# Down projection in two halves of four output tiles, with its end done tile by tile, in an autoregressive trunk on one core

## The chip, the cores and the metric

The kernel runs on one core of a Trainium2 chip. What counts is the device time of one execution in microseconds (us). Time before: 927.52 us, the median of three runs (925.98 to 929.55). Lower is better.

## What is computed

A two-layer residual trunk on 256 tokens of width 1024. Each layer is: half an FFN, a mixer, half an FFN. All FFNs are SwiGLU with an inner width of 2816. The mixer of layer 0 is latent attention beside a causal pooling mixer; that of layer 1 is a spatial gate (gMLP).

```
def _rmsnorm(x, g):
    y = x * lax.rsqrt(jnp.mean(x * x, axis=-1, keepdims=True) + EPS)
    return y * g
def _swiglu(x, w_gate, w_up, w_down):
    return (jax.nn.silu(x @ w_gate) * (x @ w_up)) @ w_down

cos, sin = _rope_tables(positions)
for layer in range(DEPTH):            # DEPTH = 2
    h = h + 0.5 * _swiglu(_rmsnorm(h, ffn_norm[layer, 0]), ...)
    hn = _rmsnorm(h, mix_norm[layer])
    if layer % 2 == 0:                # q, k, v from low rank; 8 heads; pooling; one output projection
        h = h + _mla_pool_mixer(hn, cos, sin, ...)
    else:                             # u, v = gelu(hn @ w_in); (u * mixed(v)) @ w_out
        h = h + _spatial_gating_mixer(hn, ...)
    h = h + 0.5 * _swiglu(_rmsnorm(h, ffn_norm[layer, 1]), ...)
```

## The kernel before

**Layout.** Everything is held transposed: the residual `hT` (in the trace `par_h`) has 8 tiles of 128 features by 256 tokens. Every weight passes through the core once, in chunks of 128 partitions by 1024 values (512 KB; a few are smaller). The chunks stand in one list, in the order of their use. Each is loaded into one of 5 `raw` buffers by SyncE (SP), rounded by ScalarE (ACT) to `whi` (L165), and VectorE (DVE) makes the rest `wlo = raw - whi` (L173). There are 6 pairs of `whi` and `wlo` (`PAIRS`), so a seventh chunk can be rounded only when TensorE (PE) is done with the first. Five chunks are split by GpSimd (POOL) instead.

**Matmuls.** A product with a weight is made of a rounded part and a rest on both sides. In the FFNs (`mm2`, L207 and L208) one tile of weights takes two matmuls, one of 256 columns and one of 512, the latter giving two half results in one PSUM bank. The mixers use three of 256 columns or more (`mm3`, L201 to L203). Each bank of a tile is one of eight: four in a set named `acc`, four in a set named `rot`, each set handed out in turn.

**An FFN** (`ffn`) has 11 blocks of 4 chunks in `gate_up`, which fill four banks from the normed input `x` (L207/L208 `<-x`). Blocks of even number use `acc`, of odd number `rot`. `evacuate` (L345 on ACT, L347 on DVE) and `epilogue` (L355 to L361) turn the banks into `pp`, the input of the down projection. The down stage has 22 chunks, one for each block of 128 inner features (k), each with all 8 output tiles (m), in all 8 banks: tiles 0 to 3 in `rot`, 4 to 7 in `acc`. The last two k are done tile by tile. Then `finish` adds each tile to the residual (`add`, two DVE instructions at L390), and makes from it the next stage's input: `norm_hi` (ACT, L256) and `norm_lo` (DVE, L259) write the two parts of tile m of the next `x`, `norm_sq` (ACT, L264) and POOL (L269) sum the squares. In the last FFN each tile is added and sent out instead.

**Mixers.** `even_mixer` collects its output projection in four `acc` banks, two tiles in a bank. It goes through a list `todo` of (k, m) and fills it in between the steps of attention; `pair_out` turns two heads' values (PE transposes at L858), and ACT (L859) and DVE (L860) write them as the next k of `comb`. `odd_mixer` does its output projection k by k, with all 8 tiles in four `acc` banks. Both end with `finish`, whose add is one DVE instruction at L306.

**Order.** The program's order on each engine is the order in which the Python code is written; every engine goes through its own list in order. `next_chunk` issues the loads, roundings and splits of chunks to come (three ahead, `LOOK`). `rope_tables` (L417 to L455) makes the rotary tables with some 30 small DVE instructions and a sine on ACT, after block 6 of the first FFN's gate/up stage.

## Time and profile before

| what | value |
|---|---|
| median of three runs | 927.52 us |
| the profiled execution | 928.45 us, span 926.3 us from first to last instruction |
| PE busy | 903.3 us, 98% of the span |
| DVE busy | 649.3 us, 70% |
| ACT busy | 498.2 us, 54% |
| mean granted PE clock | 0.989 |
| moved from HBM | 162.5 MB, 177 GB/s over the span |

A busy PE is not a PE at its peak: matmuls overlap, and at half clock PE counts as busy for twice as long. So the places of interest are found by the granted clock, by PE's waits, and by the distance from one matmul's start to the next. "x" with a number behind a row is its count. In a row of the timeline stand start, duration, engine, line, operation, result and inputs, and in brackets the idle time before it with what ended it.

### The profile page before, as it was taken

To read this page: it belongs to the slowest core of one execution; us is meant where nothing else is said; L and a number is where in the kernel's file an instruction comes from. 1 tells how busy PE (TensorE), PEld (TensorE's weight loads), DVE (VectorE), ACT (ScalarE), POOL (GpSimd) and SP (SyncE) were. 2 spreads that over 40 slices of the span, in tenths; PEclk is the share of its full clock that TensorE was granted. 3 is DMA by queue.
4 is the path that set the end of the run, shared out by engine and by line. 5 is a ranking of instruction groups with operands and counts; after the bars stand their busy time and mean duration, and the time that the engine had idled before them with its cause. 6 is when DMAs were issued, how large, how long until landed. Compare 5 with 4: busy or idle time off the path is not lost.

```text
span 926.3 us, 13892 instructions
## 1 busy us (share of the span) xinstructions
PE 903.3 (98%) x5320; PEld 793.7 (86%) x5320; DVE 649.3 (70%) x973; ACT 498.2 (54%) x782; POOL 98.9 (11%) x130
## 2 busy tenths in 40 slices
PE   8999899999999999999989999999999899999998
PEld 6888788889888888888878888888899888888886
DVE  7787876479875877774477777754768658777643
ACT  7555455358673655553354555543555546555430
POOL 4200000027433000000031000000220220000000
PEclk9999999999998999999989999999999999999999
DMA  8575456525353555556524555575356455555741
GB/s 284 191 248 191 135 197 239 183 88 177 114 160 114 164 193 199 194 200 228 186 93 166 198 182 183 182 242 188 98 191 207 127 167 192 182 188 199 249 137 45
DMA packets 48017, 164.45 MB, mean 178 GB/s; under 512 B 5456, under 2 KB 7760, under 8 KB 47952
## 3 DMA queue, kind: packets, MB, share of 16 engines
q1 hardware_dynamic: 47952, 163.58, 53.0%
q8 instruction: 41, 0.67, 0.3%
q14 instruction: 24, 0.20, 0.1%
HBM read 162.51 MB, written 1.05 MB: 177 GB/s over the span
## 4 chain that ended last, share of the span: by engine, by line
PE 88%; DVE 7%; POOL 1%; ACT 1%; issue 1%; DMA 1%; SPq 0%; DVEq 0%; POOLq 0%; ACTq 0%
PE acc L208 27%; PE rot L208 24%; PE acc L207 14%; PE rot L207 12%; PE acc L202 2%; PE acc L201 2%; PE acc L203 2%; DVE par_h L390 2%; DVE x L259 2%; PE rot L202 1%; PE rot L203 1%; PE rot L201 1%; DMA raw<-w_gu 1%; DVE wlo L173 1%; DVE par_h L306 1%
## 5 line engine op out<-in xcount | busy, mean ns | idle before, releaser
L173 DVE TENSOR_TENSOR wlo<-raw,whi 128x1024 fp32r<-128x1024 f32 (+2 forms) x298 | 353.8, 1229 | 102.0 <-ACT whi L165 101.9
L165 ACT CAST whi<-raw 128x1024 fp32r<-128x1024 f32 (+2 forms) x303 | 303.2, 1043 | 144.0 <-PE acc L208 117.2
L208 PE MATMUL acc<-x,whi 128*128 128x512 f32 x768 | 275.3, 401 | 0.0
L207 PE MATMUL acc<-x,wlo 128*128 128x256 f32 x768 | 219.0, 285 | 10.4 <-DVE par_h L306 4.5
L208 PE MATMUL rot<-x,whi 128*128 128x512 f32 x640 | 225.4, 396 | 0.0
L207 PE MATMUL rot<-x,wlo 128*128 128x256 f32 x640 | 179.3, 280 | 3.3 <-DVE wlo L173 3.3
L208 PEld LDWEIGHTS acc<-x,whi 128*128 128x128 f32 x768 | 147.5, 192 | 34.0
L207 PEld LDWEIGHTS acc<-x,wlo 128*128 128x128 f32 x768 | 148.0, 193 | 15.1 <-DVE par_h L306 6.7
L208 PEld LDWEIGHTS rot<-x,whi 128*128 128x128 f32 x640 | 120.7, 189 | 28.2
L208 PE MATMUL acc<-pp,whi 128*128 128x512 f32 x352 | 127.3, 396 | 0.0
L208 PE MATMUL rot<-pp,whi 128*128 128x512 f32 x352 | 127.3, 396 | 0.0
L207 PEld LDWEIGHTS rot<-x,wlo 128*128 128x128 f32 x640 | 121.1, 189 | 3.6 <-DVE wlo L173 3.6
L207 PE MATMUL acc<-pp,wlo 128*128 128x256 f32 x352 | 99.0, 281 | 0.0
L207 PE MATMUL rot<-pp,wlo 128*128 128x256 f32 x352 | 98.9, 281 | 0.0
L208 PEld LDWEIGHTS acc<-pp,whi 128*128 128x128 f32 x352 | 66.1, 188 | 16.0
L208 PEld LDWEIGHTS rot<-pp,whi 128*128 128x128 f32 x352 | 66.1, 188 | 15.9
L347 DVE TENSOR_TENSOR gu<-acc,a 128x256 f32<-128x256 f32 x96 | 34.2, 417 | 46.6 <-ACT a L345 46.4
L207 PEld LDWEIGHTS rot<-pp,wlo 128*128 128x128 f32 x352 | 66.3, 188 | 0.0
L207 PEld LDWEIGHTS acc<-pp,wlo 128*128 128x128 f32 x352 | 66.3, 188 | 0.0
L345 ACT COPY a<-acc 128x256 f32<-128x256 f32 x96 | 32.8, 372 | 62.1 <-PE acc L208 62.1
L269 POOL TENSOR_TENSOR sqsum<-sq,sq 128x256 f32<-128x256 f32 x6 | 4.6, 772 | 535.1 <-ACT sq L264 535.1
L356 ACT ACTIVATE gu<-gu 128x512 f32<-128x512 f32 x44 | 27.9, 634 | 50.5 <-DVE gu L355 50.5
(237 smaller groups left out, 1037.0 us busy)
## 6 DMA issues: line engine op xcount, KB each, us to landing
raw<-w_gu SPq DMA_DIRECT2D x172, 512.0 KB, 4.7
raw<-w_down SPq DMA_DIRECT2D x88, 512.0 KB, 4.5
raw<-ew_out SPq DMA_DIRECT2D x8, 512.0 KB, 4.0
raw<-ow_v SPq DMA_DIRECT2D x8, 512.0 KB, 3.6
raw<-ow_u SPq DMA_DIRECT2D x8, 512.0 KB, 5.1
raw<-ow_out SPq DMA_DIRECT2D x8, 512.0 KB, 4.4
raw<-ew_p SPq DMA_DIRECT2D x4, 512.0 KB, 3.9
raw<-w_gu SPq DMA_DIRECT2D x7, 256.0 KB, 5.2
```

What stands on the lines that cost most here:

```text
L165: nc.scalar.copy(hi[:, :n], r[:, :n])
L173: eng.tensor_sub(lo[:, :n], r[:, :n], hi[:, :n].bitcast(F32))
L201: nc.tensor.matmul(out, wl, xh, start=start, stop=False, skip_group_check=True)
L202: nc.tensor.matmul(out, wh, xl, start=False, stop=False, skip_group_check=True)
L203: nc.tensor.matmul(out, wh, xh, start=False, stop=stop, skip_group_check=True)
L207: nc.tensor.matmul(bank[:, 0:T], wl, x[:, 1, :], start=start, stop=False, skip_group_check=True)
L208: nc.tensor.matmul(bank, wh, x.rearrange("p s t -> p (s t)"), start=False, stop=stop, skip_group_check=True)
L259: nc.vector.scalar_tensor_tensor(s.xl[:, k, :], hT[:, k, :], pcol(s.gname, s.goff + k), s.xh[:, k, :].bitcast(F32), op0=ALU.mult, op1=ALU. ...
L345: nc.scalar.copy(a[:, i, :], bank[:, 0:T])
L347: nc.vector.tensor_add(gu[:, i, :], bank[:, T:], a[:, i, :])
L356: nc.scalar.activation(t, t, AF.Silu)
L390: nc.vector.tensor_add(hT[:, m, :], half, hT[:, m, :])
```

## The change

- **Down in halves.** A chunk of `w_down` now holds two k and four output tiles (two runs of 2 KB in a partition instead of one of 4 KB). All 11 chunks of tiles 0 to 3 come first, then the 11 of tiles 4 to 7. Each half needs four banks.
- **Bank sets dealt anew.** Each FFN is told which set its even blocks use. Half 0 takes the set of the odd blocks, half 1 that of the even blocks, and the next stage starts with the set of half 0.
- **The end tile by tile.** `finish` is cut into steps. Steps 0 to 3 are issued in half 1 after its chunks 0 to 3. The last three chunks (6 k) are fetched together (`next_chunks`, which holds back the rounding of chunks that would need one of these three's buffers), and done tile by tile with a step behind each tile. In the last FFN the steps add and send out.
- **Mixers.** In `odd_mixer` the last three k are done tile by tile, with two steps behind each second tile. In `even_mixer` what is left of `todo` after the last `pair_out` is sorted by tile, and the last k looks three chunks ahead instead of four; `finish` follows as before.
- **Rotary tables** are made in the down stage of the first FFN, after chunk 3 of half 0.

```diff
     def ffn_chunks(li):
         gu = [[w_gu[li, b, c] for c in range(4)] for b in range(NB)]
-        dn = [[w_down[li, b, j] for j in range(2)] for b in range(NB)]
-        return sum(gu, []) + sum(dn, [])
+        dn = [w_down[li, b, :, :, h * 512 : (h + 1) * 512].rearrange("j p n -> p j n")
+              for h in range(2) for b in range(NB)]
+        return sum(gu, []) + dn
...
-            while st["hi"] < min(max(st["split"] + 2, HEAD), len(chunks)):
+            while st["hi"] < min(max(st["split"] + 2, HEAD), cap or len(chunks), len(chunks)):
                 emit_hi()
...
+    def next_chunks(n, k):
+
+        cap = st["use"] + PAIRS
+        return [next_chunk(k, min(LOOK, PAIRS - 1 - i), cap) for i in range(n)]
...
+    def finisher(add, nxt):
+
+        def step(m):
+            if m < KD:
+                add(m)
+                norm_hi(nxt, m)
+            if m > 0:
+                norm_lo(nxt, m - 1)
+                norm_sq(nxt, m - 1)
+        return step
...
-    def ffn(s, nxt_args, first=False):
+    def ffn(s, nxt_args, sets, first=False):
...
-                new = rot_bank if b % 2 else acc_bank
-                banks = [new() for _ in range(4)]
+                banks = [sets[b % 2]() for _ in range(4)]
...
-                if first and b == 6:
-                    rope_tables()
...
-            ws = [next_chunk(1) for _ in range(3)]
-            for ms in (range(4), range(4, KD)):
-                for k in range(3):
-                    for m in ms:
-                        down(k, m, ws[k])
-            for k in range(3, K - 2):
-                w = next_chunk(1)
-                for m in range(KD):
-                    down(k, m, w)
-            ws = [next_chunk(1), next_chunk(1)]
-            for m in range(KD):
-                for j in range(2):
-                    down(K - 2 + j, m, ws[j])
...
+            for hf in range(2):
+                ms = range(4 * hf, 4 * hf + 4)
+                for m in ms:
+                    banks[m] = sets[1 - hf]()
+                for b in range(NB - 3 * hf):
+                    w = next_chunk(2)
+                    for j in range(2):
+                        for m in ms:
+                            down(2 * b + j, m, w)
+                    if hf == 1 and b < 4:
+                        step(b)
+                    if first and hf == 0 and b == 3:
+                        rope_tables()
+            ws = next_chunks(3, 2)
+            for m in range(4, KD):
+                for k in range(K - 6, K):
+                    down(k, m, ws[(k - K + 6) // 2])
+                step(m)
+            step(KD)
...
-            look_of = {7: 1, 6: 1, 5: 2, 4: 3, 0: 3, 1: 3, 2: 4, 3: 4}
+            look_of = {7: 1, 6: 1, 5: 2, 4: 3, 0: 3, 1: 3, 2: 4, 3: 3}
...
+            todo.sort(key=lambda t: t[1])
             fill(2 * KD * 4)
             finish(lambda m: residual(accs, m), nxt)
...
-            for k in range(KD):
+            for k in range(KD - 3):
...
+            ws = next_chunks(3, 1)
+            for m in range(KD):
+                for k in range(KD - 3, KD):
+                    out_tile(accs, m, ws[k - KD + 3], (zh[:, k, :], zl[:, k, :]), False, k == KD - 1)
+                if m % 2:
+                    step(m - 1)
+                    step(m)
+            step(KD)
...
-    s = ffn(s, ("mix", 0), first=True)
+    s = ffn(s, ("mix", 0), (acc_bank, rot_bank), first=True)
     s = even_mixer(s, ("ffn", KD))
-    s = ffn(s, ("ffn", 2 * KD))
-    s = ffn(s, ("mix", KD))
+    s = ffn(s, ("ffn", 2 * KD), (rot_bank, acc_bank))
+    s = ffn(s, ("mix", KD), (acc_bank, rot_bank))
     s = odd_mixer(s, ("ffn", 3 * KD))
-    ffn(s, None)
+    ffn(s, None, (rot_bank, acc_bank))
```

**How instructions move, three places.** First DVE where the rotary tables begin, before, in the gate/up stage (a row: line, operation, result from inputs, size; the numbers in names are buffers):

```order
L347 TENSOR_TENSOR gu_987<-acc_898,a_988 128x256
L355 TENSOR_TENSOR gu_987<-gu_987,rb_388 128x512
L357 TENSOR_TENSOR gu_987<-gu_987,rbh_390 128x512
L358 TENSOR_TENSOR gu_987<-gu_987 128x512
L361 TENSOR_TENSOR pp_212<-gu_987,pp_212 128x2x256
L419 CAST posi_1003<-pos_i 128x2
L423 TENSOR_SCALAR ang<-cst_sb,posi_1003 128x16 x2
```

The same on DVE now, in the down stage:

```order
L375 TENSOR_TENSOR pp_212<-gu_1419,pp_212 128x2x256
L177 TENSOR_TENSOR wlo_1398<-raw_1293,whi_1397 128x1024
L177 TENSOR_TENSOR wlo_1441<-raw_1335,whi_1440 128x1024
L177 TENSOR_TENSOR wlo_1463<-raw_1357,whi_1462 128x1024
L177 TENSOR_TENSOR wlo_1485<-raw_1379,whi_1484 128x1024
L435 CAST posi_1528<-pos_i 128x2
L439 TENSOR_SCALAR ang<-cst_sb,posi_1528 128x16 x2
```

Before, the tables stood right behind an epilogue, with four splits behind them; now four splits stand between the last epilogue and the tables, and only splits follow.

Second PE at the step from the second FFN's down stage (`<-pp`) to the third FFN's gate/up stage (`<-x`), before:

```order
L207 MATMUL acc_4265<-pp_3052,wlo_4619 128x256
L208 MATMUL acc_4265<-pp_3052,whi_4618 128x512
L207 MATMUL acc_4265<-pp_3052,wlo_4641 128x256
L208 MATMUL acc_4265<-pp_3052,whi_4640 128x512
L207 MATMUL acc_4817<-x_4257,wlo_4663 128x256
L208 MATMUL acc_4817<-x_4257,whi_4662 128x512
L207 MATMUL acc_4818<-x_4257,wlo_4663 128x256
L208 MATMUL acc_4818<-x_4257,whi_4662 128x512
```

The same on PE now:

```order
L216 MATMUL rot_4507<-pp_3046,wlo_4644 128x256
L217 MATMUL rot_4507<-pp_3046,whi_4643 128x512
L216 MATMUL rot_4507<-pp_3046,wlo_4666 128x256
L217 MATMUL rot_4507<-pp_3046,whi_4665 128x512
L216 MATMUL acc_4814<-x_4257,wlo_4688 128x256
L217 MATMUL acc_4814<-x_4257,whi_4687 128x512
L216 MATMUL acc_4815<-x_4257,wlo_4688 128x256
L217 MATMUL acc_4815<-x_4257,whi_4687 128x512
```

Before, the new stage's first bank was of the set that the last output tiles still filled; now the last tiles are in `rot` and the new stage begins in `acc`.

Third PE in `even_mixer` after the last pair's transposes; the chunk with `wlo_2730` is k = 2 of the output projection, the one with `wlo_2736` is k = 3, which reads what these transposes give. Before:

```order
L858 MATMUL rot_2880<-cst_sb,on_2876 128x128 x2
L201 MATMUL acc_2446<-comb,wlo_2730 128x256
L202 MATMUL acc_2446<-comb,whi_2729 128x256
L203 MATMUL acc_2446<-comb,whi_2729 128x256
L201 MATMUL acc_2446<-comb,wlo_2730 128x256
L202 MATMUL acc_2446<-comb,whi_2729 128x256
L203 MATMUL acc_2446<-comb,whi_2729 128x256
L201 MATMUL acc_2447<-comb,wlo_2730 128x256
```

The same on PE now:

```order
L874 MATMUL rot_2880<-cst_sb,on_2876 128x128 x2
L210 MATMUL acc_2445<-comb,wlo_2736 128x256
L211 MATMUL acc_2445<-comb,whi_2735 128x256
L212 MATMUL acc_2445<-comb,whi_2735 128x256
L210 MATMUL acc_2445<-comb,wlo_2736 128x256
L211 MATMUL acc_2445<-comb,whi_2735 128x256
L212 MATMUL acc_2445<-comb,whi_2735 128x256
L210 MATMUL acc_2446<-comb,wlo_2730 128x256
L211 MATMUL acc_2446<-comb,whi_2729 128x256
L212 MATMUL acc_2446<-comb,whi_2729 128x256
L210 MATMUL acc_2446<-comb,wlo_2736 128x256
```

Before, 18 matmuls of k = 2 stood between the transposes and the first matmul of k = 3; now k = 3 of tiles 0 and 1 follows the transposes at once.

More of the change, by code (lines that the diff above doesn't have):

```diff
@@ L149, in emit_dma @@
         st["dma"] += 1
-        n = chunks[i].shape[1]
+        n = int(np.prod(chunks[i].shape[1:]))
         r = wpool.tile([P, CHUNK], F32, tag="raw", name=f"raw_{i}", bufs=RAW)
@@ L153, in emit_dma @@
         if i >= HEAD:
-            nc.sync.dma_start(r[:, :n], chunks[i])
+            dst = r[:, :n]
+            if len(chunks[i].shape) == 3:
+                dst = dst.rearrange("p (k n) -> p k n", k=chunks[i].shape[1])
+            nc.sync.dma_start(dst, chunks[i])
     def emit_hi():
@@ L178, in split, with advance @@
         eng.tensor_sub(lo[:, cs], r[:, cs], hi[:, cs].bitcast(F32))
-    def advance(to_split):
+    def advance(to_split, cap=None):
         def loads():
@@ L306, in residual @@
         nc.vector.tensor_add(hT[:, m, :], bank3(accs[m // 2])[:, m % 2, :], hT[:, m, :])
-    def finish(add, nxt):
-        add(0)
-        for m in range(KD):
-            norm_hi(nxt, m)
-            if m + 1 < KD:
-                add(m + 1)
-            norm_lo(nxt, m)
-            norm_sq(nxt, m)
+    def finisher(add, nxt):
[7 more added lines that the diff above has]
+        return step
+    def finish(add, nxt):
+        step = finisher(add, nxt)
+        for m in range(KD + 1):
+            step(m)
     def out_tile(accs, m, w, a, first, last):
@@ L364, in ffn @@
             gu0 = evacuate(gate_up(0))
-            bank = acc_bank()
+            bank = sets[0]()
             def mid():
@@ L375, in ffn @@
                     early_loads()
-                if first and b == 6:
-                    rope_tables()
             nxt = norm_begin(*nxt_args) if nxt_args else None
-            banks = [rot_bank() for _ in range(4)] + [acc_bank() for _ in range(4)]
             K = 2 * NB
+            banks = {}
             def down(k, m, w):
-                ms = slice(m * P, (m + 1) * P)
-                mm2(banks[m], w[0][:, 0, ms], w[1][:, 0, ms], pp[:, k], k == 0, k == K - 1)
+                ms = slice((m % 4) * P, (m % 4 + 1) * P)
+                mm2(banks[m], w[0][:, k % 2, ms], w[1][:, k % 2, ms], pp[:, k], k == 0, k == K - 1)
             def add(m):
@@ L390, in add @@
                     nc.vector.tensor_add(hT[:, m, :], half, hT[:, m, :])
-            ws = [next_chunk(1) for _ in range(3)]
-            for ms in (range(4), range(4, KD)):
-                for k in range(3):
-                    for m in ms:
-                        down(k, m, ws[k])
-            for k in range(3, K - 2):
-                w = next_chunk(1)
-                for m in range(KD):
-                    down(k, m, w)
-            ws = [next_chunk(1), next_chunk(1)]
-            for m in range(KD):
-                for j in range(2):
-                    down(K - 2 + j, m, ws[j])
                 if nxt is None:
-                    add(m)
                     nc.sync.dma_start(outT[m], hT[:, m, :])
-            if nxt is not None:
-                finish(add, nxt)
+            step = finisher(add, nxt) if nxt is not None else (lambda m: add(m) if m < KD else None)
+            for hf in range(2):
[17 more added lines that the diff above has]
+            step(KD)
         return nxt
@@ L993, in odd_mixer @@
                 for m in range(KD):
-                    out_tile(accs, m, w, (zh[:, k, :], zl[:, k, :]), k == 0, k == KD - 1)
+                    out_tile(accs, m, w, (zh[:, k, :], zl[:, k, :]), k == 0, False)
             nxt = norm_begin(*nxt_args)
-            finish(lambda m: residual(accs, m), nxt)
+            step = finisher(lambda m: residual(accs, m), nxt)
+            ws = next_chunks(3, 1)
[4 more added lines that the diff above has]
+                    step(m - 1)
+                    step(m)
+            step(KD)
         return nxt
```

6 lines of the change are left out of this document (3 added, 3 removed).

## The prediction

> **What bounds the kernel now.** I read the page's busy times and the row of the granted clock first, then PE's own waits.
>
> ```profile
> span 926.3 us, 13892 instructions
> PE 903.3 (98%) x5320; PEld 793.7 (86%) x5320; DVE 649.3 (70%) x973; ACT 498.2 (54%) x782; POOL 98.9 (11%) x130
> PEclk9999999999998999999989999999999999999999
> ```
>
> PE is the bound nearly everywhere: 98% busy, while the next engine, DVE, has 30% to spare. But the clock dips in two of the 40 slices (the 13th and 21st), so there are stretches in which PE is busy at half speed. PE's waits in total, with count and longest:
>
> ```profile
> PE acc L207 <- DVE par_h L306: 4.5, 4, 1.1
> PE rot L207 <- DVE wlo L173: 3.3, 1, 3.3
> PE acc L207 <- DVE par_h L390: 3.1, 4, 0.9
> PE acc L293 <- POOL diag L288: 1.5, 1, 1.5
> ```
>
> They are few. `DVE par_h` is an add of an output tile to the residual, and PE waits there to write into the bank which that add still reads: `L306` at the two steps from a mixer to an FFN, `L390` at the step from the second FFN to the third. `wlo L173` is a split that came late once. Stretches of the trace around these places (length, busy time and count of PE, PEld, DVE, ACT, POOL, then granted clock, DMA share, GB/s):
>
> ```profile
> 140.00:200.00 60.00, 60.00 (x348) 52.73 (x347) 33.00 (x37) 26.24 (x31) 1.49 (x2) 1.00 0.58 190
> 25.70:29.20 3.50, 2.01 (x13) 1.57 (x12) 0.31 (x1) 1.42 (x2) 2.53 (x4) 1.00 0.89 294
> 100.90:104.30 3.40, 2.92 (x9) 2.53 (x10) 3.40 (x4) 1.71 (x2) 0.00 (x0) 0.50 0.61 166
> 274.90:278.30 3.40, 1.75 (x8) 0.79 (x6) 3.40 (x9) 3.24 (x10) 3.06 (x4) 1.00 0.11 42
> 278.30:281.80 3.50, 2.77 (x9) 2.38 (x10) 3.45 (x5) 2.42 (x5) 2.44 (x4) 0.51 0.00 0
> 281.80:285.20 3.40, 3.40 (x13) 2.92 (x12) 2.62 (x3) 1.04 (x1) 0.00 (x0) 0.50 0.52 160
> 466.10:469.50 3.40, 1.35 (x5) 0.59 (x4) 3.30 (x9) 2.18 (x6) 1.45 (x2) 1.00 0.00 0
> 472.00:476.40 4.40, 4.40 (x16) 3.73 (x15) 4.40 (x5) 3.15 (x4) 1.79 (x1) 0.51 0.36 119
> 732.30:735.70 3.40, 1.63 (x7) 0.67 (x5) 3.40 (x9) 3.24 (x9) 3.11 (x4) 1.00 0.00 0
> ```
>
> The first row is the steady state: 348 matmuls in 60.00 us, so a pair (L207 and L208) takes 0.345 us. After each place of waits the clock is 0.5 for 3.4 to 6.8 us. So a wait costs more than itself. What triggers it: stretches of 3.4 us with PE busy for 51% (274.9), 40% (466.1) and 48% (732.3) are followed by half clock; the stretch at 25.7 with 57% is not (the second and third slice of the row above show no dip).
>
> **The change part by part.** What each place costs today I take from the distance between two full-speed L208 matmuls around it, less the steady time of the pairs between them.
>
> ```profile
> 97.73 0.40 PE L208 MATMUL rot<-x,whi 128*128 128x512 f32 x1
> 104.31 0.39 PE L208 MATMUL rot<-x,whi 128*128 128x512 f32 x1
> 275.02 0.39 PE L208 MATMUL acc<-x,whi 128*128 128x512 f32 x1
> 285.18 0.40 PE L208 MATMUL acc<-x,whi 128*128 128x512 f32 x1
> 465.88 0.40 PE L208 MATMUL acc<-pp,whi 128*128 128x512 f32 x1
> 476.34 0.40 PE L208 MATMUL acc<-x,whi 128*128 128x512 f32 x1
> 732.30 0.39 PE L208 MATMUL acc<-x,whi 128*128 128x512 f32 x1
> 739.21 0.40 PE L208 MATMUL acc<-x,whi 128*128 128x512 f32 x1
> ```
>
> A, rotary tables: 6.58 us for 5 pairs (1.73), so 4.9 lost. B, first mixer to FFN: 10.16 for 12 pairs (4.14), 6.0 lost. C, second FFN to third: 10.46 for 11 pairs (3.80), 6.7 lost. D, second mixer to FFN: 6.91 for 7 pairs (2.42), 4.5 lost. Together 22.1 us.
>
> *A.* What makes the split late is on DVE:
>
> ```profile
> 93.97 0.16 DVE L419 CAST posi<-pos_i 128x2 f32<-128x2 int32 x1
> 100.11 3.49 DVE L173 TENSOR_TENSOR wlo<-raw,whi 128x1024 fp32r<-128x1024 f32 x3
> L173 DVE TENSOR_TENSOR wlo<-raw,whi 128x1024 fp32r<-128x1024 f32 (+2 forms) x298 | 353.8, 1229 | 102.0 <-ACT whi L165 101.9
> L165 ACT CAST whi<-raw 128x1024 fp32r<-128x1024 f32 (+2 forms) x303 | 303.2, 1043 | 144.0 <-PE acc L208 117.2
> ```
>
> From 93.97 to 100.11, 6.1 us, DVE makes tables, the sine on ACT among them, and the next split waits behind. In the gate/up stage DVE also has the epilogues. In the down stage (row 140.00:200.00) it is busy 33.0 of 60.0 us: a chunk takes PE 8 pairs, 2.76 us, and DVE one split of 1.23. As six pairs of buffers exist, a split can run when PE starts on the chunk five before it; 6.1 us of delay leave 13.8 - 1.0 (rounding) - 1.2 - 6.1, over 5 us. ACT's roundings wait behind the sine as long, with the same room. So A goes whole: 4.9. If that cover were gone, it would cost up to 4.9 again.
>
> *B, C, D.* The next stage now starts in the other set of banks, whose readers are done long before; and all but the last one or two tiles are added and normed while PE works on. What is late next would be the next input: PE needs the last tile of `x` only after 7 of 8 k, 28 pairs or 9.7 us into the stage. A step's cost on DVE:
>
> ```profile
> 468.97 0.87 DVE L390 TENSOR_TENSOR par_h<-acc,par_h 128x256 f32<-128x256 f32 x2
> 469.76 0.82 DVE L259 SCALAR_TENSOR_TENSOR x<-par_h,x 128x256 fp32r<-128x256 f32 x1
> ```
>
> At most 1.7 us a tile; in the tail PE spends 6 k, so 6 pairs or 2.07 us, on each. There DVE has four such steps (6.8) and one split that had to wait for the tail's start (1.2), 8.0 in PE's 8.3 us. As the last step starts only with the last tile, DVE ends some 2 us after PE, over 7 us before that tile is needed. ACT, busy 26.2 of 60.0 us in the down stage, gets no work that it did not have, only earlier. In half 1 a step and a split, 2.9 us at most by these rows against 2.76, eat 0.6 us over four chunks out of a lead of several chunks. The held-back rounding of the fourth chunk of the next stage needs 1.0 + 1.2 us after the end, and three chunks, 8.3 us, cover it; without the cover it costs what rival 2 says. In the mixers a step has one add instead of two. So the four places give 22.1 us.
>
> *A new wait, in B.* Sorting `todo` puts k = 3 straight behind the transposes whose result it reads:
>
> ```profile
> 269.65 0.38 PE L858 MATMUL rot<-cst_sb,on 128*128 128x128 f32 x2
> 270.09 0.36 ACT L859 CAST comb<-rot 128x256 fp32r<-128x256 f32 x1
> 270.48 0.42 DVE L860 TENSOR_TENSOR comb<-rot,comb 128x256 fp32r<-128x256 f32 x1 [0.94 <-ACT comb L859]
> 272.94 0.76 DVE L306 TENSOR_TENSOR par_h<-acc,par_h 128x256 f32<-128x256 f32 x2 [0.90 <-PE acc L203]
> ```
>
> Today 18 matmuls of k = 2 hide ACT's and DVE's copies. Now PE ends the transposes at 270.03, starts one matmul when the rounded part is there (270.45), and goes on when the rest is there (270.90). The wait is at least 0.75 us (both gaps) and at most 1.3 (from the transposes' start); I take 1.0. Behind it, in PE's queue, stands the whole rest of the projection, so it counts in full. The last row: the adds of tiles 0 and 1 begin when both tiles of their bank are done; that stays so, and now the banks end one after the other while PE goes on.
>
> *Smaller ones.* E, the end:
>
> ```profile
> 921.65 0.40 PE L208 MATMUL acc<-pp,whi 128*128 128x512 f32 x1
> 920.31 3.25 DVE L390 TENSOR_TENSOR par_h<-acc,par_h 128x256 f32<-128x256 f32 x8
> 207.42 0.43 PE L202 MATMUL rot<-wlo,x 128*128 128x416 f32 x1 [0.42 <-DVE wlo L173]
> ```
>
> PE ends at 922.05, the adds at 923.56, since a tile takes DVE 0.81 us and PE 0.69. With 2.07 us a tile DVE no longer lags: the last add ends some 0.9 us after PE, a gain of 0.6. Four output transfers go earlier on SP's queue; the loads behind them are five buffers ahead. F: the wait at 207.42, behind `finish`, goes: 0.4. At the step from the third FFN to the second mixer PE does not wait today, so nothing is gained.
>
> *Half rows.* Loads of `w_down` have twice as many runs, of 2 KB. No row has just these; the nearest are the first loads, of 1 to 2 KB runs:
>
> ```profile
> 3.00:9.00 6.00, 4.57 (x24) 3.53 (x23) 2.99 (x6) 3.19 (x7) 0.00 (x0) 1.00 0.84 245
> raw<-w_gu SPq DMA_DIRECT2D x7, 256.0 KB, 5.2
> ```
>
> 0.84 at 245 GB/s is 0.0034 a GB/s, against 0.0031 (0.58 at 190) with 4 KB runs: 12% more. From below: nothing. From above: each 2 KB run takes as long as a 4 KB one, share 1.16 instead of 0.58. I take 12%, near which the row lies: share 0.65, hidden.
>
> Sum: 22.1 + 0.6 + 0.4 - 1.0 = 22.1 us. The profiled execution took 928.45 (span 926.3 and 2.1 around it): 906.4. The median of the runs shown is 0.9 lower, so 905.5; I say **906**.
>
> **The clock and the skill.** The stretches above show half clock after waits of at most 1.1 us each, where they add up to half of 3.4 us; the new wait of 1.0 us leaves PE 70% busy, more than the 57% that kept the clock. The Trainium skill, "TensorE: Matmul & The Clock Gate", section "HAM oscillation — how this bites in real kernels", states as a rule that PE must not idle for more than about 3.4 us. By that rule only A's wait comes near; the trace differs at B, C and D, and decides. For the new wait rule and rows agree on no loss, and the sum would be the same 906 by either.
>
> **The rivals.** 1: the new wait halves the clock, as shorter waits together did. For it: those were no longer than 1.1 us each. Against it: it is a single one, and 57% was enough at 25.7. It costs half of one or two stretches of 3.4 us, 1.7 to 3.4: 908 to 909. 2: the hand-over is not hidden, since DVE reaches the next stage's fourth chunk late. For it: DVE is busy 3.3 to 3.4 of 3.4 us at these steps today. Against it: the 5 us of room above. Price: rounding and split in full, 2.3 us, plus half of 3.4 us of half clock, 4.0 at each of the three steps into an FFN: 918. 3: A is moved, not removed: 906 + 4.9 = 911. 4, on the other side: the half rows make the down stage wait for DMA. It decides where the share reaches 1, that is where a chunk's transfer takes 1.72 times today's time. At twice (the upper bound) a chunk takes 1.16 x 2.76 = 3.2 us, 0.44 more than PE, 88 times: 39 us, less the 22 gained, so 945, slower. Against it: 12% in the nearest row. 5: the change does not do what it says, the waits of B, C and D stay since banks still meet: 906 + 17.2 = 923. The order speaks against it: `acc` follows `rot`.
>
> **How the numbers follow.** Forecast 906: 74%. Rival 1: 8%. Rival 2: 8%. Rival 3: 5%. Rival 4: 2%. Rival 5: 3%. The forecast's own bounds: the new wait 0.75 to 1.3, the four places some 2 us up or down by the runs' own spread (926.0 to 929.6) and another phase of the clock's stretches. With rivals 1 and 3 taken in and the others left out: 903 to 912. A difference under 0.5% (4.6 us) is about what a measurement of this kernel cannot tell from none. Rival 5 is the only case within it, rival 4 the only one slower: faster 95%, same 3%, slower 2%.
>
> **What would show it.** Right: no wait of PE on `par_h` or on the split behind the tables; granted clock 1.00 past the start; one new wait of about 1 us of PE on `comb` at some 265 us; DMA share in the down stages near 0.65; last add under 1 us after PE's end. Wrong: a row of half clock after the new wait (rival 1); PE waiting on `wlo` some 8 us into an FFN (rival 2) or in the first down stage (3); PE waiting on loads with a share near 1 (4).

## The result, and the profile after

The changed kernel takes 912.71 us (median of four executions, 910.51 to 912.91), the kernel before 927.78 (four executions beside it, 925.98 to 929.55): a ratio of 0.983, with a 95% interval from 0.981 to 0.986. It is faster by 15.1 us, a small change (1.7%) that is clear of the noise. Two executions on record, one of the kernel before (1256.55 us) and one in run 12 (2269.0 us), lie far above all others and are left out below. Forecast were 906 us and at most 912, so some 7 us of the expected 22 are missing.

The page of the changed kernel: the first line, the busy times, and the row of the granted clock.

```profile
span 910.8 us, 13887 instructions
PE 899.7 (99%) x5320; PEld 790.6 (87%) x5320; DVE 645.5 (71%) x973; ACT 496.4 (55%) x782; POOL 99.5 (11%) x130
PEclk9999999999999999999999999999999999999999
```

The two slices with a lower clock are gone, and PE is busy for 99% of the span. PE's waits, the four longest (total, times, longest; the lines of code have moved by some ten):

```profile
PE acc L216 <- DVE wlo L182: 2.4, 3, 1.8
PE acc L302 <- POOL diag L297: 1.4, 1, 1.4
PE acc L1030 <- DVE wu L1026: 1.0, 1, 1.0
PE acc L210 <- ACT comb L875: 0.6, 1, 0.6
```

No wait on `par_h` is left, nor the one behind the rotary tables. The first row is the start of the kernel, where the first pieces of weights are split; the last one is the new wait that was forecast. The stretches of the changed kernel at the four places and in its first down stage (length, busy time and count of PE, PEld, DVE, ACT, POOL, then granted clock, DMA share, GB/s):

```profile
97.00:103.80 6.80, 6.80 (x41) 5.91 (x40) 4.73 (x9) 2.61 (x6) 0.00 (x0) 1.00 0.86 296
272.80:279.60 6.80, 6.80 (x41) 5.91 (x40) 6.77 (x10) 6.60 (x12) 5.18 (x6) 1.00 0.09 27
460.10:466.90 6.80, 6.80 (x40) 5.88 (x39) 5.28 (x7) 5.65 (x8) 2.21 (x3) 1.00 0.14 47
719.60:726.40 6.80, 6.80 (x41) 5.92 (x40) 5.62 (x8) 6.02 (x12) 3.43 (x5) 1.00 0.05 9
135.40:197.40 62.00, 62.00 (x353) 53.87 (x352) 42.06 (x80) 28.09 (x39) 3.65 (x4) 1.00 0.56 191
```

PE is busy without a gap at full clock, with 40 or 41 matmuls in each 6.8 us; before there were 5 to 13 in 3.4 us. At the step from the second FFN to the third, the last 512 column matmul of the one, the eleventh of the other, and the adds of the last tile at the kernel's end:

```profile
459.90 0.39 PE L217 MATMUL rot<-pp,whi 128*128 128x512 f32 x1
463.78 0.40 PE L217 MATMUL acc<-x,whi 128*128 128x512 f32 x1
907.13 0.89 DVE L402 TENSOR_TENSOR par_h<-rot,par_h 128x256 f32<-128x256 f32 x2 [1.24 <-PE rot L217]
```

11 pairs in 3.88 us: nothing but steady work. So every wait that was to go has gone. Where is the rest? The last window says it: the prediction has 348 matmuls in 60.00 us of the first down stage before, here there are 353 in 62.00, which is fewer per time, at full clock and without a wait. And the trace of before had this all along, in stages that the prediction did not look at. The third FFN's down stage, then 100 us of gate/up of the second and of the third FFN, all of the kernel before:

```profile
600.00:660.00 60.00, 60.00 (x341) 52.11 (x340) 32.57 (x36) 26.32 (x31) 1.47 (x2) 1.00 0.59 193
300.00:400.00 100.00, 100.00 (x579) 87.49 (x578) 79.41 (x113) 60.32 (x94) 0.00 (x0) 1.00 0.54 180
492.00:592.00 100.00, 100.00 (x568) 86.77 (x567) 77.73 (x111) 58.67 (x92) 0.00 (x0) 1.00 0.53 179
```

341 where the same work in the first FFN has 348; 568 where the second FFN has 579. The changed kernel has the lower count in its second FFN too:

```profile
300.00:400.00 100.00, 100.00 (x568) 86.78 (x567) 76.66 (x108) 57.66 (x90) 0.00 (x0) 1.00 0.57 191
```

(The counts of a window include matmuls that its edges cut, so I take paces from the starts.) From the start of one 512 column matmul to that of the next it is either 346.7 ns in the mean or 353.3, with nothing between, from one end of a stage to the other in both of these traces. I call these the fast and the slow rhythm of PE. A gate/up stage (from the middle of its second block on) has 304 pairs: 105.4 or 107.4 us. A down stage has 176: 61.0 or 62.2. The lengths of these stages, from start to start (f marks the fast rhythm; the down stage of the fourth FFN is 0.2 shorter as its last pair is not counted):

| kernel | gate/up of FFN 1, 2, 3, 4 | down of FFN 1, 2, 3, 4 |
|---|---|---|
| before | 110.23 f (with the tables' stretch), 105.40 f, 107.41, 105.40 f | 61.01 f, 63.25 (with waits at its end), 62.17, 61.95 |
| changed | 107.41, 107.41, 107.41, 107.41 | 62.17, 62.17, 62.17, 61.94 |

Before, four of the eight stages ran in the fast rhythm in the profiled execution; in the changed kernel none did. That is 3 x 2.01 + 1.16 = 7.2 us, the missing part. The rest adds up: 22.7 us gained at the places of waits, at the start and the end, less 7.2, are the 15.5 us between the spans, 926.3 and 910.8. (The places gained 4.8, 5.9, 6.6 and 4.4 us and the end 0.55, as worked out further below; the start was 0.7 shorter, the first mixer 0.25 longer.)

### The profile page after: what moved, and what is told of

Its sections match the earlier page's. It is cut to its first block, busy times and chain, and to the rows that moved or that the text cites. A ratio compares the mean times of both kernels' runs of the same rounds, so it can differ in the third digit from the quotient of the medians.

```text
span 910.8 us, 13887 instructions
## 1 busy us (share of the span) xinstructions
PE 899.7 (99%) x5320; PEld 790.6 (87%) x5320; DVE 645.5 (71%) x973; ACT 496.4 (55%) x782; POOL 99.5 (11%) x130
## 4 chain that ended last, share of the span: by engine, by line
PE 95%; DVE 1%; POOL 1%; issue 1%; DMA 0%; ACT 0%; SPq 0%; DVEq 0%
PE rot L217 27%; PE acc L217 26%; PE rot L216 14%; PE acc L216 13%; PE acc L211 3%; PE acc L210 3%; PE acc L212 2%; PE rot L210 2%; PE rot L212 2%; PE rot L211 2%; DMA raw<-w_gu 0%; PE rot L973 0%; POOL diag L297 0%; DVE wlo L182 0%; PE rot L821 0%
## 5 line engine op out<-in xcount | busy, mean ns | idle before, releaser
L217 PE MATMUL rot<-x,whi 128*128 128x512 f32 x704 | 249.8, 399 | 0.0
L217 PE MATMUL acc<-x,whi 128*128 128x512 f32 x704 | 249.7, 398 | 0.0
L216 PE MATMUL acc<-x,wlo 128*128 128x256 f32 x704 | 198.3, 282 | 2.4 <-DVE wlo L182 2.4
L216 PE MATMUL rot<-x,wlo 128*128 128x256 f32 x704 | 197.9, 281 | 0.0
L217 PEld LDWEIGHTS rot<-x,whi 128*128 128x128 f32 x704 | 132.3, 188 | 32.6
L217 PEld LDWEIGHTS acc<-x,whi 128*128 128x128 f32 x704 | 132.3, 188 | 32.2
L216 PEld LDWEIGHTS acc<-x,wlo 128*128 128x128 f32 x704 | 133.0, 189 | 3.6 <-DVE wlo L182 3.5
L216 PEld LDWEIGHTS rot<-x,wlo 128*128 128x128 f32 x704 | 133.0, 189 | 0.0
L217 PE MATMUL rot<-pp,whi 128*128 128x512 f32 x352 | 124.5, 397 | 0.0
L217 PE MATMUL acc<-pp,whi 128*128 128x512 f32 x352 | 124.5, 397 | 0.0
L217 PEld LDWEIGHTS acc<-pp,whi 128*128 128x128 f32 x352 | 66.1, 188 | 16.4
L217 PEld LDWEIGHTS rot<-pp,whi 128*128 128x128 f32 x352 | 66.1, 188 | 16.4
L359 ACT COPY a<-rot 128x256 f32<-128x256 f32 x88 | 30.0, 372 | 57.7 <-PE rot L217 57.7
L361 DVE TENSOR_TENSOR gu<-rot,a 128x256 f32<-128x256 f32 x88 | 31.5, 419 | 36.3 <-ACT a L359 36.3
```

What stands on the lines that cost most here:

```text
L216: nc.tensor.matmul(bank[:, 0:T], wl, x[:, 1, :], start=start, stop=False, skip_group_check=True)
L217: nc.tensor.matmul(bank, wh, x.rearrange("p s t -> p (s t)"), start=False, stop=stop, skip_group_check=True)
L359: nc.scalar.copy(a[:, i, :], bank[:, 0:T])
L361: nc.vector.tensor_add(gu[:, i, :], bank[:, T:], a[:, i, :])
```

## Experiments

Two questions: is the slow rhythm made by the change (other banks, half rows, norm steps beside the matmuls), or is it a state into which a stage falls? And what is it that takes longer?

**1. The changed kernel once more.** Nothing is edited.

> The changed kernel once more, nothing edited. Reading so far: no wait and no half clock is left, yet a pair of FFN matmuls takes 353.3 ns in all eight FFN stages, where before four of the eight ran at 346.6 ns (gate/up of FFNs 1, 2, 4 and the first down stage). Theory 1, two rhythms, of which a stage falls into one by its entrance: 910 to 913 again, and where a gate/up stage (312 pairs) falls into the fast one the run is 2.0 to 2.1 us shorter, a down stage (176 pairs) 1.2 us. Theory 2, the change itself makes the pair slower (bank sets, half rows, norm steps beside the matmuls): all eight stages at 353.3 ns in every profile, 912.6 to 912.9 each time.

910.73 us median (four executions, 910.51 to 910.91), 0.984 of before, interval 0.979 to 0.989. In its profile gate/up of FFN 3 is fast, 105.39 us, the other seven stages are slow. The count in that stage:

```profile
480.00:580.00 100.00, 100.00 (x579) 87.47 (x578) 79.45 (x112) 60.48 (x94) 0.00 (x0) 1.00 0.54 181
```

The same program with the same work ran one stage at 579 in 100 us instead of 568. That stage was 2.0 us shorter, the execution 1.7 us (910.91 against 912.56). So theory 2, that the change itself makes the pair slower, cannot be the whole: the changed kernel can run fast.

**2. The kernel before once more.**

> The kernel before once more. If its four fast stages (gate/up of FFNs 1, 2, 4, first down stage) were the chance of one execution: another set of fast stages, in the mean fewer than four of eight, as the kernel with the tables alone had none. If something in the kernel before makes them fast: the same four again.

931.26 us, one execution. Its stretches, in the order gate/up of FFN 1, down of FFN 1, gate/up of FFN 2, gate/up of FFN 3, down of FFN 3:

```profile
40.00:90.00 50.00, 50.00 (x285) 43.41 (x284) 39.45 (x53) 28.80 (x46) 1.45 (x1) 1.00 0.63 212
140.00:200.00 60.00, 60.00 (x342) 52.09 (x341) 31.90 (x36) 25.32 (x30) 0.38 (x1) 1.00 0.59 197
300.00:400.00 100.00, 100.00 (x569) 86.81 (x568) 76.98 (x111) 57.40 (x92) 0.00 (x0) 1.00 0.54 181
496.00:596.00 100.00, 100.00 (x579) 88.15 (x578) 79.43 (x113) 60.11 (x94) 0.00 (x0) 1.00 0.53 180
602.00:662.00 60.00, 60.00 (x347) 52.69 (x346) 33.55 (x38) 27.18 (x32) 1.59 (x3) 1.00 0.60 196
```

Now the third FFN is fast in both stages, and every stage that was fast in the first profile begins slowly. So which stages are fast changes from one execution of the kernel to the next.

Gate/up of FFN 1 holds one thing more. Up to its wait behind the rotary tables a pair takes 353.3 ns from start to start, behind the wait 346.7, to the end of the stage (in 30 us of it 175 matmuls, where the first row above has 285 in 50 us):

```profile
106.00:136.00 30.00, 30.00 (x175) 26.27 (x174) 23.98 (x34) 18.64 (x29) 0.00 (x0) 1.00 0.56 189
```

So the rhythm can change within a stage, here at a pause and the half clock behind it. It need not: in the first profile this stage was fast before the same wait and behind it.

**3. The rotary tables alone moved**, in the kernel before.

```diff
-                if first and b == 6:
-                    rope_tables()
...
+                if first and k == 6:
+                    rope_tables()
```

> The kernel before with the rotary tables alone moved into its down stage (behind k = 6). Term A of the prediction: 4.9 us less, 922.6, no half clock in FFN 1. Theory 1: 4.9, and 2.0 or 1.2 us more or less where a stage of FFN 1 falls into the other rhythm. Theory 2: FFN 1 keeps 346.6 ns in both stages, since it has the old banks, rows and steps. A third theory, that pauses or half clock put PE into the fast rhythm: gate/up of FFN 1 stays as it was up to the old place of the tables (fast from 22 us on), and gate/up of FFNs 2 and 4 stay fast.

923.38 us median of ten executions (921.31 to 929.66), beside 926.81 for before; the ratio's interval, 0.995 to 1.001, takes in no change at all and ends just short of the 4.9 that were forecast, so the times alone do not show A. In its profile (of the longest execution, 929.66) the wait behind the tables and the half clock of FFN 1 are gone, and gate/up of FFN 1 takes 107.41 instead of 110.23, not 105.4, since it ran slow. All eight stages did: with the old banks, rows and steps (against theory 2), and behind the same waits at the later FFNs (against the third theory, that pauses always bring the fast rhythm).

This profile holds one thing more. The same step from the first mixer to the FFN, 3.4 us each, then the second of the four windows at the step from the second FFN to the third:

```profile
272.60:276.00 3.40, 1.77 (x8) 0.81 (x6) 3.40 (x9) 3.24 (x10) 3.04 (x4) 1.00 0.10 39
276.00:279.40 3.40, 2.63 (x15) 2.31 (x16) 3.35 (x5) 3.02 (x6) 2.49 (x4) 1.00 0.00 0
464.40:467.80 3.40, 2.05 (x6) 0.95 (x5) 3.33 (x8) 2.14 (x6) 1.56 (x3) 0.72 0.00 0
```

In the prediction, 51% busy at this place (1.75 of 3.40) is followed by half clock; here 52% (1.77) is not, and the step costs 2.7 us less (20.9 us from the FFN's start to the middle of its second block, 23.6 before). At the next step the clock does fall (0.72 in the mean of this row). So the share of busy time in such a stretch alone does not decide. The Trainium skill, "TensorE: Matmul & The Clock Gate", section "What's actually happening", describes the clock gate's window as 3413 ns long and free-running, so that it matters where in it the work lands; the two traces are consistent with that, though they do not show where the window begins. Where the window begins may be one more reason why executions of the kernel before differ: the shortest on record, 919.48 us, had a mean granted clock of 0.996, the longest, 934.47 us, one of 0.988.

**4. Kicks.** One pair in 32 of each gate/up stage (from its block 2 on) and one in 16 in the larger part of each down stage is issued in another way (the expectation's "one in 16" for gate/up is a slip): in FFNs 1 and 4 with the 512 column matmul first, in FFN 2 with that matmul cut in two, in FFN 3 with the 256 column one cut in two.

```diff
+        if kind == "swap":
+            nc.tensor.matmul(bank, wh, xx, start=start, stop=False, ...)
+            nc.tensor.matmul(bank[:, 0:T], wl, x[:, 1, :], start=False, stop=stop, ...)
+            return
```

> The changed kernel with one pair in 16 of the gate/up stages (from block 2 on) and one in 16 of the down stages issued in another way, same products: in FFNs 1 and 4 the 512 column matmul first, in FFN 2 the 512 column matmul as two of 256, in FFN 3 the 256 column one as two of 128. Theory 1 (rhythm by the entrance): behind some of these pairs the spacing switches between 353.3 and 346.6 ns and stays there until the next one, in the same stage, with the same banks, loads and work of the other engines. Theory 2 (the change makes the pair slower): 353.3 ns between all of them. Cost of the odd pairs: nothing for the swap, some 20 ns for a cut.

The run takes 911.17 us (one execution). From one swapped pair of a gate/up stage to the next there are 32 pairs. The 512 column matmuls of the first five swaps in FFN 1 (start, duration; `L217` is here the swapped matmul's own line):

```profile
38.56 0.40 PE L217 MATMUL acc<-x,whi 128*128 128x512 f32 x1
49.65 0.39 PE L217 MATMUL rot<-x,whi 128*128 128x512 f32 x1
60.95 0.40 PE L217 MATMUL acc<-x,whi 128*128 128x512 f32 x1
72.05 0.39 PE L217 MATMUL rot<-x,whi 128*128 128x512 f32 x1
83.34 0.40 PE L217 MATMUL acc<-x,whi 128*128 128x512 f32 x1
```

The distances are 11.09, 11.30, 11.10 and 11.29 us: 32 pairs at 346.7, 353.3, 346.7, 353.3 ns. It goes on so through all nine swaps of FFN 1, and again in FFN 4. In FFN 2 the stretches go slow, slow, fast, three times over; in FFN 3's gate/up stage a cut of the 256 columns never helps, in its down stage it brings the fast rhythm three times out of eight. In the down stages of FFNs 1, 2 and 4 nothing did; that of FFN 2 began fast, and its first altered pair ended it. With the same banks, loads and neighbours, one pair of matmuls can switch the pace of all that follow, up to the next such pair: the rhythm is a state in which PE's stream of matmuls stays. Theory 2, that every pair of the changed kernel costs more, has fallen. Whether the change makes the slow rhythm more frequent is another question, taken up further below.

**5. Other orders of the same matmuls.** FFN 1 with the 512 column matmul first throughout; FFNs 2 and 4 two tiles together (256, 256, 512, 512), FFN 3 four together.

```diff
+            for t in todo[i : i + n]:
+                lo(t)
+            for t in todo[i : i + n]:
+                hi(t)
```

> The changed kernel with another order of the same matmuls throughout an FFN: FFN 1 the 512 column matmul first in each pair, FFNs 2 and 4 two tiles together (256, 256, 512, 512), FFN 3 four tiles together. In the mixers a matmul of 256 columns takes 120.0 ns and one of 512 226.7 ns in steady rows, which makes 346.7 a pair. Theory 1: the slow rhythm adds 6.7 ns a pair to this by how short and long matmuls alternate, so the grouped orders may have a rhythm of their own, 346.7 if the loss comes with each change from long to short only, or less loss in FFN 3 (a quarter as many changes): 346.7 to 348.3 there. Theory 2: 353.3 in all orders, since banks, loads and the other engines are as in the changed kernel.

905.71 us (one execution). Two together: 348.4 ns a pair in gate/up and 351.3 in the down stage, in both FFNs; four together 350.0 and 350.9. The 512 column matmul first: 346.7 in gate/up, 353.3 in the down stage. The sum that the expectation starts from is that of the mixers' rows in the changed kernel, first with 512 columns, then with 256 (all matmuls alike, so each stands at its own pace):

```profile
650.00:666.00 16.00, 16.00 (x72) 13.23 (x72) 9.71 (x8) 8.72 (x9) 1.08 (x2) 1.00 0.71 244
702.00:718.00 16.00, 16.00 (x136) 16.00 (x135) 9.99 (x16) 7.73 (x12) 1.07 (x2) 1.00 0.66 215
```

From start to start 226.7 and 120.0 ns: 346.7 together, the fast rhythm. The slow one adds 6.7 ns to every pair.

**6. The swapped order in all four FFNs, and 7. still others:** matmuls of two tiles side by side, so that no two in a row write one bank (down of FFN 1, gate/up of FFN 2); eight together (FFN 3); 256, 512, 512, 256 (FFN 4).

```diff
+                for i in range(4):
+                    lo(todo[g + (i + 1) % 4])
+                    hi(todo[g + i])
```

> The changed kernel with the 512 column matmul ahead of the 256 column one in every pair of all four FFNs. Shown by the runs so far: a single pair in this order switches a gate/up stage between 353.3 and 346.6 ns, and a gate/up stage wholly in this order ran at 346.6. If the order sets the rhythm: four gate/up stages at 346.6, 8.0 us less than all slow, 904.6; the down stages stay at 353.4. If it was the entrance again: a mix of 346.6 and 353.0 between the four gate/up stages, 905 to 912.

> The changed kernel with further orders of the same matmuls. FFN 1: gate/up 512 first, down with the 256 column matmul of a tile and the 512 column one of another tile side by side (no two in a row in one bank). FFN 2: the same the other way about. FFN 3: eight of 256, then eight of 512. FFN 4: 256, 512, 512, 256. If two matmuls in a row in one bank make the slow rhythm: 346.7 ns where banks alternate (down of FFN 1, gate/up of FFN 2). If each change between short and long costs: eight together 346.7 + 1.7 = 348.3, and 256, 512, 512, 256 like two together, 348.4 in gate/up and 351.3 in down. If neither: 353.3 or 346.6 by chance.

The swapped order gives 910.62 us (four executions, 910.07 to 912.52; 0.983 of before, 0.979 to 0.987), and in the profiled one all eight stages are slow:

```profile
310.00:390.00 80.00, 80.00 (x455) 69.35 (x454) 60.50 (x85) 45.22 (x71) 0.00 (x0) 1.00 0.55 188
```

So its fast stage in run 5 was chance, and the order does not set the rhythm. In run 7 (909.37 us) banks that alternate change nothing (353.4 and 353.0); eight together give 349.1 and 351.6, and 256, 512, 512, 256 gives 348.4 and 351.4, as two together. My expectation of 348.3 for eight was too simple: the loss does not fall with the number of changes between short and long.

**8. and 9. What the pair waits for.** Parts of the work are left out, so the results are not the reference's: fewer columns streamed by the short matmul, and fewer weight columns (64 or 32 of 128) loaded for the one or the other, in all but the first and last k. The two runs take 897.75 and 857.50 us (one execution each).

```diff
+            nc.tensor.matmul(bank[0:rows_lo, 0:cols], wl[:, 0:rows_lo], x[:, 1, 0:cols], ...)
+            nc.tensor.matmul(bank[0:rows_hi, :], wh[:, 0:rows_hi], x.rearrange("p s t -> p (s t)"), ...)
```

> The changed kernel with work left out of each FFN's pairs (but the first and last k): FFN 1 loads 64 instead of 128 weight columns for the 256 column matmul, FFN 2 the same for the 512 column one, FFN 3 streams 128 instead of 256 columns in the short matmul, FFN 4 192. Theory M1, the weight load of the next matmul sets how soon it can start (matmuls of 1 column follow each other at 111.7 ns in the row of the norm's sums): FFN 3 111.7 + 226.7 = 338 a pair, FFN 4 338 to 347, no gain as large as the columns; FFN 2, whose load under the short matmul is halved, loses the slow rhythm, 346.7 or less; FFN 1 (its load lies under the long matmul) as before, 353.3. Theory M2, columns alone set the time (13.3 ns and 0.417 ns a column): FFN 3 293, FFN 4 320, FFNs 1 and 2 unchanged, 346.7 or 353.3.

> The changed kernel with work left out of each FFN's pairs (but the first and last k): FFN 1 128 columns in the short matmul and 64 weight columns for the long one, FFN 2 the same and 64 weight columns for both, FFN 3 all 256 columns and 64 weight columns for both, FFN 4 all 256 and 32 weight columns for the long one. If the load of the long matmul's weights is what bounds the short one (M1) and goes by its columns: FFNs 1 and 2 60 + 226.7 = 287 a pair, FFNs 3 and 4 340.0 (113.3 + 226.7). If a load takes the same time whatever its columns: FFNs 1 and 2 338 to 343 as with 128 weight columns, FFNs 3 and 4 346.7 or 353.3.

| columns of the short matmul | weight columns for the short / the long one | pair in gate/up, ns | in down, ns |
|---|---|---|---|
| 256 (the kernel) | 128 / 128 | 346.7 or 353.3 | 346.7 or 353.3 |
| 256 | 64 / 128 | 346.8 | 346.7 |
| 256 | 128 / 64 | 340.0 | 346.7 |
| 256 | 64 / 64 | 340.0 | 350.4 |
| 256 | 128 / 32 | 340.0 | 350.0 |
| 192 | 128 / 128 | 344 | 342.2 |
| 128 | 128 / 128 | 340.0 | 343.3 |
| 128 | 128 / 64 | 287 and 300, block by block in turn | 293.3 |
| 128 | 64 / 64 | 290 | 290.6 |

The rows behind two of these: 128 columns with full weights in the down stage, and 128 columns with 64 weight columns for both.

```profile
590.00:610.00 20.00, 20.00 (x118) 17.41 (x117) 10.53 (x14) 9.03 (x11) 0.00 (x0) 1.00 0.67 225
367.00:407.00 40.00, 40.00 (x274) 27.26 (x272) 27.55 (x31) 22.02 (x26) 2.31 (x2) 1.00 0.80 263
```

118 in 20 us and 274 in 40: halving the short matmul's columns saves 10 to 13 ns of a slow pair, though 128 columns fewer would be half of the 120.0 that 256 take; halving the load as well saves 60. So the next matmul's weight load bounds a short matmul of 128 columns (theory M1), and the columns alone do not (M2, 293 and 320, falls). The Trainium skill, "TensorE: Matmul & The Clock Gate", section "LDWEIGHTS (loading the stationary operand)", gives a load's time by its weight columns alone, as columns divided by 1.2, in ns: 107 for 128 and 53 for 64. The runs come near the first of these: where the short matmul is cut to 128 columns, the time beyond the long one's 226.7 is 113 to 117 ns with 128 weight columns. With 64 it is 60 to 73, near the 67 that M2's figures give for 128 columns alone, so these rows do not test the 53. (With 64 weight columns a matmul also writes 64 output rows instead of 128; no run tells this from the load.) M1 missed three rows: 346.7 with half of the load under the long matmul, where 353.3 was expected (in one run this may also be the fast rhythm by chance), and 350 in the down stage, where 340 was expected, with both loads halved and with a quarter of the long one's. So loads have a part in the pace, but these rows do not explain what keeps a rhythm going.

**10. The changed kernel without the sorting**, which brought the new wait.

```diff
-            todo.sort(key=lambda t: t[1])
```

> The changed kernel without the sorting of the output projection's list in the first mixer, so that the matmuls of k = 2 cover the last transposes as in the kernel before. By the prediction's new wait: no wait of PE on comb, 1.0 us less between the last transposes and the end of the projection (0.6 as the trace of the changed kernel has it), but then the banks of tiles 0 to 5 end later, so the steps of finish run behind PE's end; since the next FFN starts in the other banks and needs tile 7 only 9.7 us later, no wait comes back: 0.6 to 1.0 us faster, give or take 2.0 for each gate/up stage and 1.2 for each down stage that falls into the other rhythm.

909.44 us. PE's wait on `comb` is gone; the list begins

```profile
PE acc L216 <- DVE wlo L182: 2.1, 3, 1.3
PE acc L302 <- POOL diag L297: 1.4, 1, 1.4
```

From the start of the first down stage to that of the second FFN it is 136.36 us against 137.45, 1.09 less, and the start of that FFN is 0.2 longer (17.92 against 17.73, to the middle of its second block), with no wait in it. Another gate/up stage was fast, that of FFN 2, 2.0 us.

**11. and 12. Two versions that use this.** Both leave the sorting out. One alters a single pair in each of the eight FFN stages, as in run 4; the other puts two tiles together in all of them.

```diff
+                                "swap" if (b, k, i) == (2, 3, 1) else None)
...
+                    "cut256" if (k, m) == (3, 1) else None)
```

> The changed kernel without the sorting, and with one pair of matmuls altered in each of the eight FFN stages: in gate/up the pair of block 2, k = 3, tile 1 has its 512 column matmul first; in the down stage that of k = 3, tile 1 has its 256 columns as two matmuls of 128. If the rhythm is a state that such a pair switches, and the stages start in the slow one as most did: behind the pair 270 pairs of each gate/up stage and 163 of each down stage run at 346.7 instead of 353.3 ns, 4 x (1.8 + 1.1) = 11.6 us, and 1.1 for the sorting: 912.6 - 12.7 = 899.9. A stage that starts fast is switched to slow, and loses 1.8 us. If the state is not set by it, or falls back by itself: 911.5.

> The changed kernel without the sorting, and with two tiles together (256, 256, 512, 512) in all FFN stages. As in FFNs 2 and 4 of the run with these orders: 348.4 ns a pair in gate/up and 351.3 in the down stage, in each of the stages and each execution, since this order showed one rhythm only: 105.9 and 61.85 us a stage, 4 x (1.5 + 0.3) = 7.3 us less than all slow, 1.1 less for the sorting: 904.2, with a spread below 1 us between executions. If it too has two rhythms: stages of 107.4 among them.

One pair: 902.43 us (four executions, 900.25 to 903.77), 0.973 of before, interval 0.968 to 0.978. In its profile, of the execution that took 900.25, every stage is fast behind the altered pair: 105.4 to 105.6 and 61.2 us. Gate/up of FFN 2 and the down stage of FFN 4:

```profile
310.00:390.00 80.00, 80.00 (x463) 69.90 (x463) 62.15 (x87) 45.99 (x72) 0.00 (x0) 1.00 0.57 192
860.00:890.00 30.00, 30.00 (x175) 26.39 (x174) 13.46 (x18) 7.35 (x7) 0.00 (x0) 1.00 0.26 85
```

The forecast for this run was 899.9. Eight pairs out of 2112, which do the same work in another form, are worth some 11 us from one profiled execution to the other (912.56 to 900.25, less 1.1 for the sorting), and some 9 by the medians (912.71 to 902.43, less the same). FFN 2 was in the fast rhythm from the start of its second block, and the altered pair did not end it. The other three executions are 1.9 to 3.5 us longer; that fits one or two stages which did not switch, but no profile of them shows it.

Two together: 904.43, 903.94 and 904.32 us (forecast 904.2), 0.974 of before, interval 0.970 to 0.979. All four gate/up stages take 105.89 to 105.92, all four down stages 61.84 or, without the last pair, 61.61:

```profile
310.00:390.00 80.00, 80.00 (x462) 69.78 (x461) 61.78 (x87) 46.38 (x73) 0.00 (x0) 1.00 0.55 186
860.00:890.00 30.00, 30.00 (x173) 26.18 (x172) 13.97 (x17) 9.10 (x9) 0.00 (x0) 1.00 0.34 105
```

This order had one rhythm in each kind of stage, in the four stages of run 5 and the eight here, a little slower than the fast one, and its executions lie within 0.5 us. Both are faster than the kernel before and than the changed kernel (910.51 to 912.91 us in its eight executions).

## Why the prediction was right and wrong

**The step that failed is the sum.** "The profiled execution took 928.45: 906.4" takes 22.1 us from that execution and lets everything else stand. This holds only if a pair takes the same time in both. The prediction read 0.345 us from one window, in the first down stage, and took it for the kernel's steady state. It was the fast one of two rhythms (346.7 ns by the starts), in which this execution had four of eight stages; the profiled execution of the changed kernel had none, and 7.2 us went there. So the pace of PE where it waits for nothing is the term that the sum put at nothing without a reason. Three more windows of the same trace, one for each like stage, would have shown it, and would have made the range wider by the rhythm alone: 4 x 2.0 + 4 x 1.16 = 12.6 us lie between all fast and all slow.

**Probably it was not luck alone.** Of the 48 FFN stages in the six profiles of runs with the usual order, 8 were fast from end to end: 6 of the 24 with the old down stage (before twice, the tables alone) and 2 of the 24 with the new one (changed twice, without sorting). The times point the same way, by an estimate. The span times the mean granted clock leaves out what half clock cost. For the profiled execution of before this is 926.3 x 0.989 = 916.1 us, so some 923.3 if its four fast stages had been slow too. The median of 26 other executions of before is 917.4, the highest 922.2, so the middle one owes some 6 us to the fast rhythm, nearly as much as the profiled one. The changed kernel has a span of 910.8 with all stages slow and a median span of 909.1 over eight executions, so some 2 us. (The clock is on record to three digits, which is 0.5 us.) So the fast rhythm seems to come less often in the changed kernel. With less half clock in most executions of before (a clock of 0.992 in the middle one, 0.989 in the profiled one), that would be why the medians too differ by 15 us and not by 22. The cause is not shown. The rhythm changed at a pause in run 2, and the changed kernel has fewer pauses, but no run tests whether that sets the odds.

**A to D were right, place by place.** A: gate/up of FFN 1 held 4.8 us (110.23 less the 105.4 of a fast stage) over its work, 4.9 predicted; nothing is left. B, C, D: from an FFN's start to the middle of its second block it was 23.64, 23.32 and 22.12 us, now 17.73, 17.81 and 17.73; with the 1.1 that the second down stage lost at its end, the gains are 5.9, 6.6 and 4.4, against 6.0, 6.7 and 4.5. The half clock went with the waits.

**The new wait was right:** 1.0 predicted, 1.09 by run 10, which takes the whole sorting out. The profile's own row says 0.6, so here the row of a wait understates what the new order costs. The clock held at 1.00 behind it, as predicted, so rival 1 did not come.

**E was right:** from the end of PE's last matmul to the end of the span it is 3.7 us, before 4.25; 0.55, 0.6 predicted. F's wait is gone, but the first mixer as a whole is 0.25 longer (75.28 against 75.03): 1.09 for the new wait, less 0.4 for F, leaves 0.4 of gain that I have no row for. The start of the kernel was 0.7 shorter in this execution; in the others it varied by as much.

**Half rows were sized too high, without effect:** DMA share 0.56 in the first down stage, 0.58 before, where 0.65 was predicted. Runs of 2 KB cost nothing that these windows show, and rival 4 had no ground.

**The rivals.** None of the five came. Their prices went by waits and clock; none was about the pace of PE where it waits for nothing. The result lies near the price of rival 3 (911), and only the trace tells that it is another cause: the wait behind the tables is gone.

**What stays open:** what chooses the rhythm at a stage's entrance, whether the change itself makes the fast one rarer, why the down stage resists the swap, and why it stands at 350 ns with both loads halved. The runs show that the rhythm is a state, that a single pair can switch it and that it can change at a pause, and that a short matmul of 128 columns waits, as far as they tell, for the next weight load.

## What to carry to other kernels

Before a sum is made against one profiled execution, compare the pace of like stages within it: matmuls per window, at full clock and without waits; if they differ, the pace is a term of its own, with its own range. A short matmul can be bound by the next weight load, so that fewer columns save little (here 10 to 13 ns of 353 for half of the columns), and the order of short and long matmuls is a knob worth a run: here two tiles together gave one pace in each kind of stage, and one altered pair a stage gave the shortest time. A gain at the places of waits can be whole and still not be the gain in time.

## What the runs showed of the hardware that was not expected

- PE keeps one of two rhythms for 60 to 110 us on end, 346.7 or 353.3 ns for a pair of a 256 and a 512 column matmul, at full granted clock and without any wait. One pair issued in another way can switch it (11.09 and 11.30 us, in turn, for the same 32 pairs), and it changed once at a pause (353.3 ns before the wait behind the tables, 346.7 behind it, in run 2). Other orders of the same matmuls have paces of their own, from 348.3 to 351.6 ns.
- With 128 weight columns to load for the next matmul, a pair takes 340 to 344 ns whether its short matmul streams 128 or 192 columns, against 346.7 or 353.3 with 256. With 64 weight columns and 128 streamed it takes 287 to 300.
- Two stretches with PE busy for 51% and 52% of 3.4 us at the same step of the program: one is followed by half clock, the other is not.
